# Mixer: weight casts behind an mLSTM head's decays, and tail steps of the modulation queue in the last units of output projections

## The chip, the cores and the metric

One NeuronCore of a Trainium2 chip runs the whole layer as one program. The metric is the device time of one execution in microseconds (us), the median of three runs. Engines are named as in the profile: PE (TensorE, matmuls), ACT (ScalarE), DVE (VectorE), POOL (GpSimd) and SP (SyncE, which here issues nearly all transfers). Each engine takes its own instructions in order, and waits on semaphores of others.

## The reference, cut to what matters

One layer for 256 tokens, width 2048, feed-forward width 5632, all in float32:

```python
ada = silu(c) @ w_ada + b_ada                 # nine vectors of 2048: sh1, sc1, g1, ... g3
sh1, sc1, g1, sh2, sc2, g2, sh3, sc3, g3 = split(ada, 9)
h = swiglu(modulate(x, sh1, sc1), ffn1_w_in, ffn1_w_out)
x = layernorm(ALPHA * x + 0.5 * (1 + g1) * h, ln1_g, ln1_b)
h = token_mixer(modulate(x, sh2, sc2), ...)   # 8 Fox attention heads, 4 mLSTM heads, w_out
x = layernorm(ALPHA * x + (1 + g2) * h, ln2_g, ln2_b)
h = swiglu(modulate(x, sh3, sc3), ffn2_w_in, ffn2_w_out)
x = layernorm(ALPHA * x + 0.5 * (1 + g3) * h, ln3_g, ln3_b)
```

`modulate(x, sh, sc)` is a layer norm without parameters, times (1 + sc), plus sh. An mLSTM head weighs its products q.k by decays: exponentials of differences of accumulated gates, cut to the causal triangle.

## The kernel before, in words

**Matrix products.** A float32 product is made of three matmuls in a reduced format (`mm3`, L398 to L401): each operand is split into `hi`, its cast, and `lo`, the rest. Activations are split once. Weights are split as they come: `load_w` (L368) issues a 1 MB transfer on SP into one of three `raw` buffers (L374), ACT casts each half of it to `hi` (L150, six buffers) and DVE subtracts to get `lo` (L151, six buffers). PE then uses both. So SP, ACT and DVE must keep ahead of PE, and each is in order. The argument `behind` of `load_w` names an instruction after which the cast and the subtraction of that tile must be issued.

**Stages.** FFN1 (in, out projection `f1`), a boundary with the layer norm and the next modulation, the mixer, its out projection `mx`, a second boundary, FFN2 (columns 2 to 9 in two halves, `fh` over the first half of the rows, `gf` and `fs` over the second), its out projection `f2`, and the last layer norm.

**Mixer.** In order: the o-gate columns (`mo`), the v columns (`fv`, `mv` with 520 columns, then `mv` with 512), the mLSTM q and k (`m`), the Fox q and k of heads 4 to 7 (`fb`, `fbk`), those of heads 0 to 3 (`fa`, `fak`), the rest of the Fox v (`fv`), then `mx`. Each of these has four units of one `raw` tile. Behind each unit stands `step()`: `pump(R_MX)` and up to three steps of side work (attention heads, mLSTM heads). `form_a_four` (L1111) makes the q and k blocks. `mlstm_head` (L1292) issues for a head: the matmuls `gb` (gate row) and `sps` (q.k), four ACT instructions `dm` (L1306, L1307: the decays), four DVE multiplies (L1308, L1309), and a step later the matmuls `nps`. `sps` has one buffer that all four heads share. Heads 0 and 1 lie in and behind the last `fb` unit, heads 2 and 3 between the `fbk` units.

**Modulation vectors.** The nine vectors of `ada` are computed beside all that, by `AdaQueue`, in units named (vector, column block). A unit has sixteen *rows*: a 512 KB transfer on SP (L184) into one of two buffers `ar`, and a DVE multiply-add (L163 for the first, L165). Then it has *tail* steps: `ahi` on ACT, `alo` on DVE, the pair of matmuls `bc` (L178) that sum over the partitions, and for shift and scale the DVE steps `dg`, reduce and add (L195 to L199). `pump(n)` adds n to `owed`, makes one tail step if there is one, and then one row for each whole number in `owed`. A new unit with a buffer of its own isn't started while a tail of such a unit is pending, and then the rows stay owed. `need(n)` makes steps at once until n units are done, and sets `owed` to zero each time it finds them not done. Rates per unit: 1.2 in FFN1, 1 in its out projection, 1.42 in the mixer and in `mx`, 1.05 and 0.6 in FFN2.

In the last column group of an out projection (`lastg`), the last four units aren't pumped. At the end of `f1`, `finish1` calls `need(6)`; the tail of unit (3, 3), which held back the next unit, isn't done by then, 3.25 rows are owed, and they are forgotten. `need(12)` ahead of `gf` likewise finds the tail of (6, 3) not done, and forgets 0.79.

**Order.** The program is written in an order, and a scheduler then sets the order of each engine from priorities and its own idea of durations; `tc.issue_after` and `tc.manual_schedule` bind it at some places.

Of the kernel before, what the change touches and what calls it, by code (L numbers as in the profile page):

```python
# [9 lines left out]
AF = mybir.ActivationFunctionType  # L10
# [22 lines left out]
def layer_kernel(  # L33
# [8 lines left out]
    V, S, G_, PE, SP = nc.vector, nc.scalar, nc.gpsimd, nc.tensor, nc.sync  # L42
# [98 lines left out]
    @contextmanager  # L141
    def pinned():
        with ExitStack() as s:
            for i in pin.values():
                s.enter_context(tc.issue_after(i))
            yield
# [67 lines left out]
    class AdaQueue:  # L214
# [19 lines left out]
        def row(self):  # L234
# [14 lines left out]
                self.rows = None  # L249
            return True  # L250

        def pump(self, n):
            self.owed += n
            with pinned():
                if self.tails:
                    self.tail()
            while self.owed >= 1:
                with pinned():
                    if not self.row():
                        break  # L260
                self.owed -= 1
# [169 lines left out]
    def out_proj(w, rows, nk, tag, npump, finish, before=None, turned=False, spare=None, fine=None):  # L431
# [12 lines left out]
        for width in (1024, 512, 512):  # L444
# [55 lines left out]
            for i, u in enumerate(us):  # L500
                hs = []
                if before:
                    before(u * kn)
                into = spare() if spare and lastg and i == nu - nheld else None
                for k in range(u * kn, u * kn + kn, 2):
                    hs += rows(k)
                for kk, hi, lo in load_w(w[u * kn * P:(u + 1) * kn * P, col:col + width], kn, width,
                                         f"{tag}o{col}_{u}", into=into):
                    arg = (u * kn + kk, *hs[kk], hi, lo)
                    if lastg and i >= nu - nheld or not lastg and i == nu - 1:  # L510
                        held.append(arg)
                    else:
                        for a in range(2):
                            if a and lastg and fine is not None:
                                products(a, [arg], nk - nheld * kn - 1)
                            else:
                                products(a, [arg])
                if not lastg and i == nu - 1:

                    late += [add_up(a, bs=(b,)) for b in range(nb) for a in range(2)]  # L520
                    products(0, held)
                    catch_up(2)
                    products(1, held)
                else:
                    catch_up(2)
                if not lastg or i < nu - 4:
                    npump()
            if lastg:
                catch_up(99)
                if fine is None:  # L530
                    finish(lambda a: products(a, held), add_up, st)
                else:
                    for _ in add_up(1, stats=False):
                        pass
                    outs = [mm_tile(f"o_{tag}last{c}") for c in range(2)]
                    finish(lambda a: half_products(outs) if a else products(0, held),
                           lambda a: add_halves(outs) if a else add_up(0), st)
            else:
                col += width
# [423 lines left out]
    W = w_in[0]  # L963
# [98 lines left out]
    def step():  # L1062
        pump(R_MX)
        advance(NP)
# [5 lines left out]


    emptied = [None]


    def cols_form_b(c0, col, ws, use, name, four=False):
# [35 lines left out]
    def form_a_four(c0, name, before_last=lambda: None):  # L1111
        ps = [mm_tile(f"pr_{name}{i}", True) for i in range(2)]
        for u in range(4):
            if u == 3:
                before_last()
            for k4, hi, lo in load_w(W[u * 512:(u + 1) * 512, c0:c0 + 512], 4, 512, f"{name}{u}"):
                k = 4 * u + k4
                for f in range(4):
                    fs = slice(f * P, (f + 1) * P)
                    mm3(ps[f // 2][:, f % 2 * T:(f % 2 + 1) * T], hi[:, fs], lo[:, fs], xhi[:, k, :], xlo[:, k, :],  # L1120
                        k + f % 2 == 0, k + f % 2 == KD)
            step()
        return [ps[f // 2][:, f % 2 * T:(f % 2 + 1) * T] for f in range(4)]

# [168 lines left out]
    def mlstm_head(o, h):  # L1293
        yield from wait(["gates", "conv1"] + [f"head{h - 2}"] * (h > 1) + [f"o{h - 1}"] * (h % 2))
        if h % 2:
            yield True
        qm, km = o[:, 0, :], o[:, 1, :]
        gb = aux_tile(f"gb{h}")
        sps = [fifth_tile(f"sps{h}")[:, :T], gb[:, T:T + P]]
        dm = mx.tile([P, T + P], F32, tag="dm", bufs=2, name=f"dm{h}")  # L1300
        PE.matmul(gb[:, :T], sel(h), ng, start=True, stop=True)
        for i in range(2):
            PE.matmul(sps[i], km[:, i * P:(i + 1) * P], qm[:, i * P:], start=True, stop=True)
        for i in range(2):
            d = dm[:, i * T:T + i * P]
            S.activation(d, gb[:, i * P:T], AF.Relu, bias=nacol[:, i, h:h + 1])  # L1306
            S.activation(d, d, AF.Exp, scale=-1.0)  # L1307
            V.tensor_tensor(out=d[:, :P], in0=d[:, :P], in1=triu1[:, :P], op=ALU.mult)  # L1308
            V.tensor_tensor(out=d, in0=sps[i], in1=d, op=ALU.mult)  # L1309
        done.add(f"o{h}")  # L1310
        yield
        yield True
        nps = [aux_tile(f"nps{h}{tt}") for tt in range(2)]
        for tt in range(2):
            PE.matmul(nps[tt][:, :MV + 1], dm[:, tt * P:(tt + 1) * P], yM[h][:, 0, :MV + 1],
                      start=True, stop=tt == 0)
        PE.matmul(nps[1][:, :MV + 1], dm[:, T:], yM[h][:, 1, :MV + 1], start=False, stop=True)
        for tt in range(2):
            dn = sm.tile([P, 2], F32, tag="dn", bufs=4, name=f"dn{h}{tt}")
            V.scalar_tensor_tensor(out=dn[:, 0:1], in0=nps[tt][:, MV:MV + 1], scalar=-1.0, in1=em[:, tt, h:h + 1],  # L1320
                                   op0=ALU.mult, op1=ALU.max)
            V.tensor_tensor(out=dn[:, 0:1], in0=nps[tt][:, MV:MV + 1], in1=dn[:, 0:1], op=ALU.max)
            V.reciprocal(dn[:, 1:2], dn[:, 0:1])
            S.mul(hm(h)[:, tt, :], nps[tt][:, :MV], dn[:, 1:2])
            S.activation(nps[tt][:, :MV], hm(h)[:, tt, :], AF.Square, accum_out=ss[:, tt, h:h + 1])
        done.add(f"head{h}")
        yield
# [183 lines left out]
    for j in range(2, 10):  # L1511
        if j == 8:
            for _ in mb:
                pass
        if j == 7:
            mb = late_features(2, 11)
        ps = half_in(j, 0, "fh")
        for f in range(2):
            i = 2 * j + f
            S.copy(hT[:, i, :], ps[f][:, :T])  # L1520
            S.copy(hT[:, i + 16, :], ps[f][:, T:])
# [71 lines left out]
```

## Time and profile before

| | us |
|---|---|
| median of three runs (lowest, highest) | 1929.29 (1928.31, 1930.26) |
| the profiled execution | 1927.28 |
| its span | 1925.6 |
| PE busy | 1891.5 (98%) |
| DVE busy | 1483.4 (77%) |
| ACT busy | 953.7 (50%) |
| mean granted clock of PE | 0.995 |

A row of a timeline has start, duration, engine, line, operation, out<-in, shapes, and how many of the kind follow each other; in brackets the idle time of the engine ahead of it, and what ended that. In a row of a window table each engine's busy time stands with its number of instructions, then PE's granted clock, the share of the DMA engines, and GB/s. Times of a transfer run from issue to landing.

### The profile page before, as it was taken

The numbers are of one execution on the slowest core, as the hardware profiler recorded it, in microseconds if no ns is written. First come the engines' busy times: TensorE is split into PE (matmuls) and PEld (weight loads), VectorE is DVE, ScalarE is ACT, GpSimd is POOL, SyncE is SP. The second block draws the span as 40 slices with busy tenths as digits, with TensorE's granted clock in tenths as the row PEclk, the third lists the DMA queues.
The fourth block names the chain that finished last, engine by engine and source line by source line (L and its number), as shares of the span: only waits on it lengthen the run. The fifth ranks groups of instructions, "written<-read, shape, count | busy, mean of one in ns | idle before, by whom it ended". The sixth has DMA issues, their size and how long they took to land.

```text
span 1925.6 us, 32413 instructions
## 1 busy us (share of the span) xinstructions
PE 1891.5 (98%) x13133; PEld 1724.6 (90%) x13133; DVE 1483.4 (77%) x1847; ACT 953.7 (50%) x1359; POOL 59.7 (3%) x88
## 2 busy tenths in 40 slices
PE   6999999999999999999999999999999999999997
PEld 3999999999988887699989886999999999988886
DVE  6788989877789898888988887867766655555776
ACT  3554454444454555845655645565444444444562
POOL 1111100000000000100000000000000000000000
PEclk9999999999999999999999999999999999999999
DMA  9978969999898787499988883987777766755552
GB/s 359 375 262 313 328 218 296 337 331 306 266 339 296 267 301 236 138 321 317 319 300 272 315 300 114 338 282 246 262 248 260 246 213 196 240 184 189 196 196 89
DMA packets 283662, 510.92 MB, mean 265 GB/s; under 512 B 10962, under 2 KB 134514, under 8 KB 282488
## 3 DMA queue, kind: packets, MB, share of 16 engines
q1 hardware_dynamic: 275640, 480.53, 73.4%
q0 software_dynamic: 7872, 28.32, 4.4%
q8 instruction: 103, 1.69, 0.4%
q14 instruction: 47, 0.39, 0.1%
HBM read 506.71 MB, written 2.10 MB: 264 GB/s over the span
## 4 chain that ended last, share of the span: by engine, by line
PE 84%; DVE 7%; DMA 5%; issue 2%; ACT 1%; SPq 0%; DVEq 0%; POOL 0%; ACTq 0%
PE gu_f L401 8%; PE gu_f L400 8%; PE gu_f L399 8%; PE o_f L399 6%; PE o_f L401 6%; PE o_f L400 6%; PE s L400 4%; PE s L399 4%; PE s L401 4%; DMA ar<-in_w_ada_dram 3%; PE fs L401 1%; PE fs L399 1%; PE fs L400 1%; PE o_mx L399 1%; PE o_mx L401 1%
## 5 line engine op out<-in xcount | busy, mean ns | idle before, releaser
L165 DVE SCALAR_TENSOR_TENSOR acc<-ar,csil,acc 128x1024 f32<-128x1024 f32 (+1 forms) x167 | 211.4, 1267 | 52.2 <-DMA ar<-in_w_ada_dram 51.5
L400 PE MATMUL s<-xlo_f,hi_s 128*128 128x256 f32 x768 | 213.6, 278 | 1.2 <-DVE xlo_f L331 1.2
L399 PE MATMUL s<-xhi_f,hi_s 128*128 128x256 f32 x768 | 213.4, 279 | 0.0
L401 PE MATMUL s<-xhi_f,lo_s 128*128 128x256 f32 x768 | 213.3, 278 | 0.0
L401 PE MATMUL gu_f<-xhi_f,lo_f2i 128*128 128x256 f32 x768 | 212.0, 276 | 0.0
L399 PE MATMUL gu_f<-xhi_f,hi_f2i 128*128 128x256 f32 x768 | 212.0, 276 | 0.0
L400 PE MATMUL gu_f<-xlo_f,hi_f2i 128*128 128x256 f32 x768 | 212.0, 276 | 0.0
L151 DVE TENSOR_TENSOR lo_f2i<-raw_f2i,hi_f2i 128x1024 fp32r<-128x1024 f32 x96 | 117.4, 1224 | 92.4 <-ACT hi_f2i L150 92.4
L401 PE MATMUL gu_f<-xhi_f,lo_f1i 128*128 128x256 f32 x640 | 176.7, 276 | 0.0
L399 PE MATMUL gu_f<-xhi_f,hi_f1i 128*128 128x256 f32 x640 | 176.7, 276 | 0.0
L400 PE MATMUL gu_f<-xlo_f,hi_f1i 128*128 128x256 f32 x640 | 176.7, 276 | 0.0
L150 ACT CAST hi_f2i<-raw_f2i 128x1024 fp32r<-128x1024 f32 x96 | 100.8, 1050 | 135.4 <-PE gu_f L400 124.6
L150 ACT CAST hi_s<-raw_s 128x1024 fp32r<-128x1024 f32 x96 | 100.6, 1052 | 130.3 <-PE s L400 93.4
L400 PEld LDWEIGHTS s<-xlo_f,hi_s 128*128 128x128 f32 x768 | 145.5, 189 | 1.5 <-DVE xlo_f L331 1.5
L401 PEld LDWEIGHTS s<-xhi_f,lo_s 128*128 128x128 f32 x768 | 145.4, 189 | 0.0
L399 PEld LDWEIGHTS s<-xhi_f,hi_s 128*128 128x128 f32 x768 | 144.9, 189 | 0.0
L399 PEld LDWEIGHTS gu_f<-xhi_f,hi_f2i 128*128 128x128 f32 x768 | 144.2, 188 | 0.2
L400 PEld LDWEIGHTS gu_f<-xlo_f,hi_f2i 128*128 128x128 f32 x768 | 144.2, 188 | 0.2
L401 PEld LDWEIGHTS gu_f<-xhi_f,lo_f2i 128*128 128x128 f32 x768 | 144.2, 188 | 0.0
L151 DVE TENSOR_TENSOR lo_f2o<-raw_f2o,hi_f2o 128x1024 fp32r<-128x1024 f32 x86 | 105.2, 1223 | 43.3 <-ACT hi_f2o L150 43.3
L165 DVE SCALAR_TENSOR_TENSOR gate<-ar,csil,gate 128x1024 f32<-128x1024 f32 (+1 forms) x94 | 117.5, 1251 | 25.4 <-DMA ar<-in_w_ada_dram 25.2
L151 DVE TENSOR_TENSOR lo_s<-raw_s,hi_s 128x1024 fp32r<-128x1024 f32 x96 | 115.5, 1219 | 27.4 <-ACT hi_s L150 27.2
(478 smaller groups left out, 5511.6 us busy)
## 6 DMA issues: line engine op xcount, KB each, us to landing
ar<-in_w_ada_dram SPq DMA_DIRECT2D x227, 512.0 KB, 5.4
raw_f2i<-in_ffn_w_in_dram SPq DMA_DIRECT2D x48, 1024.0 KB, 5.2
raw_s<-in_ffn_w_in_dram SPq DMA_DIRECT2D x47, 1024.0 KB, 7.6
raw_f1o<-in_ffn_w_out_dram SPq DMA_DIRECT2D x44, 1024.0 KB, 7.3
raw_f2o<-in_ffn_w_out_dram SPq DMA_DIRECT2D x44, 1024.0 KB, 5.1
raw_f1i<-in_ffn_w_in_dram SPq DMA_DIRECT2D x40, 1024.0 KB, 7.4
ar<-in_w_ada_dram POOLq DMA_DIRECT2D x48, 512.0 KB, 6.9
raw_mxo<-in_w_out_dram SPq DMA_DIRECT2D x16, 1024.0 KB, 6.0
```

Source lines behind the costliest of these rows:

```text
L150: S.copy(hi, src)
L151: return V.tensor_tensor(out=lo, in0=src, in1=hi.bitcast(F32), op=ALU.subtract)
L165: V.scalar_tensor_tensor(out=acc, in0=raw, scalar=csil[:, k:k + 1], in1=acc, op0=ALU.mult, op1=ALU.add)
L399: PE.matmul(o, ah, bh, start=start, stop=False)
L400: PE.matmul(o, ah, bl, start=False, stop=False)
L401: PE.matmul(o, al, bh, start=False, stop=stop)
```

## The change

A method `end_step` makes one tail step and no row. It is called in the last four units of an out projection's last column group, and once more in each of the last two columns of `fh`. And the casts and subtractions of a q or k block's unit are issued behind the decays of the mLSTM head that was recorded two units before.

```diff
+        def end_step(self):
+            if self.tails:
+                with pinned():
+                    self.tail()
+
         def pump(self, n):
             self.owed += n
-            with pinned():
-                if self.tails:
-                    self.tail()
+            self.end_step()
             while self.owed >= 1:
...
                 if not lastg or i < nu - 4:
                     npump()
+                else:
+                    ada.end_step()
...
     emptied = [None]
+    decays = [None, None]
...
-            for k4, hi, lo in load_w(W[u * 512:(u + 1) * 512, c0:c0 + 512], 4, 512, f"{name}{u}"):
+            for k4, hi, lo in load_w(W[u * 512:(u + 1) * 512, c0:c0 + 512], 4, 512, f"{name}{u}",
+                                     behind=decays[0]):
...
+            decays[:] = decays[1], None
             step()
...
-            S.activation(d, d, AF.Exp, scale=-1.0)
+            decays[1] = S.activation(d, d, AF.Exp, scale=-1.0).ins
...
         ps = half_in(j, 0, "fh")
+        if j >= 8:
+            ada.end_step()
```

All engines have as many instructions as before, and up to the first `mv` units (some 850 us into the span) they stand in the same order. The lists below are the order of the built programs; a digit right behind the letters of a name is left out (`ar_1_2` is row 2 of unit (6, 1), `bc_3_0` belongs to unit (6, 3)), and the last number of a name is the buffer's. Lines of the new program are 3 to 8 higher from L249 on.

ACT, at the mLSTM heads 0 and 1 (`dm` is written by the decays, `hi_fbk` by the casts for `fbk`), before:

```order
L150 CAST hi_fbk_10448<-raw_fbk_10446 128x1024
L150 CAST hi_fbk_10476<-raw_fbk_10446 128x1024
L150 CAST hi_fbk_10540<-raw_fbk_10538 128x1024
L150 CAST hi_fbk_10568<-raw_fbk_10538 128x1024
L1306 ACTIVATE dm_10354<-gb_10352,nacol 128x256
L1306 ACTIVATE dm_10354<-gb_10352,nacol 128x128
L1307 ACTIVATE dm_10354<-dm_10354 128x256
L1307 ACTIVATE dm_10354<-dm_10354 128x128
L150 CAST hi_fbk_10621<-raw_fbk_10619 128x1024
L1383 ACTIVATE qs_10711<-pr_fb_10121 128x256
L150 CAST hi_fbk_10649<-raw_fbk_10619 128x1024
L1306 ACTIVATE dm_10432<-gb_10430,nacol 128x256
```

and now:

```order
L1314 ACTIVATE dm_10366<-gb_10364,nacol 128x256
L1314 ACTIVATE dm_10366<-gb_10364,nacol 128x128
L1315 ACTIVATE dm_10366<-dm_10366 128x256
L1315 ACTIVATE dm_10366<-dm_10366 128x128
L150 CAST hi_fbk_10457<-raw_fbk_10455 128x1024
L150 CAST hi_fbk_10485<-raw_fbk_10455 128x1024
L1391 ACTIVATE qs_10720<-pr_fb_10140 128x256
L1314 ACTIVATE dm_10441<-gb_10439,nacol 128x256
L1314 ACTIVATE dm_10441<-gb_10439,nacol 128x128
L1315 ACTIVATE dm_10441<-dm_10441 128x256
L1315 ACTIVATE dm_10441<-dm_10441 128x128
L150 CAST hi_fbk_10549<-raw_fbk_10547 128x1024
```

The decays of head 0 moved ahead of the four casts for the first two units of `fbk`, and those of head 1 ahead of the second pair.

ACT again, at heads 2 and 3 (`yM` and `nps` end head 0), now:

```order
L1332 ACTIVATE yM_8728<-nps_10516,dn_10521 128x256
L1332 ACTIVATE yM_8728<-nps_10517,dn_10527 128x256
L1333 ACTIVATE nps_10516,ss<-yM_8728 128x256
L1333 ACTIVATE nps_10517,ss<-yM_8728 128x256
L1314 ACTIVATE dm_10535<-gb_10533,nacol 128x256
L1314 ACTIVATE dm_10535<-gb_10533,nacol 128x128
L1315 ACTIVATE dm_10535<-dm_10535 128x256
L1315 ACTIVATE dm_10535<-dm_10535 128x128
L150 CAST hi_fbk_10630<-raw_fbk_10628 128x1024
L150 CAST hi_fbk_10658<-raw_fbk_10628 128x1024
L1391 ACTIVATE qs_10724<-pr_fb_10141 128x256
```

Before, the casts `hi_fbk` of this unit stood ahead of head 2's L1306, and its L1307 behind `yM` and `nps`; now both casts stand behind all of that.

SP, the transfers around `mv`'s 512-column units, before:

```order
L184 DMA ar_1_0_9268<-in_w_ada_dram 128x2x512
L374 DMA raw_mv_0_9358<-in_w_in_dram 128x4x512
L184 DMA ar_1_1_9341<-in_w_ada_dram 128x2x512
L184 DMA ar_1_2_9392<-in_w_ada_dram 128x2x512
L374 DMA raw_mv_1_9401<-in_w_in_dram 128x4x512
L184 DMA ar_1_3_9445<-in_w_ada_dram 128x2x512
L374 DMA raw_mv_2_9466<-in_w_in_dram 128x4x512
L184 DMA ar_1_4_9448<-in_w_ada_dram 128x2x512
L374 DMA raw_mv_3_9519<-in_w_in_dram 128x4x512
L374 DMA raw_m_9572<-in_w_in_dram 128x4x512
```

and now:

```order
L184 DMA ar_1_0_9140<-in_w_ada_dram 128x2x512
L184 DMA ar_1_1_9209<-in_w_ada_dram 128x2x512
L377 DMA raw_mv_0_9377<-in_w_in_dram 128x4x512
L184 DMA ar_1_2_9288<-in_w_ada_dram 128x2x512
L184 DMA ar_1_3_9291<-in_w_ada_dram 128x2x512
L377 DMA raw_mv_1_9430<-in_w_in_dram 128x4x512
L184 DMA ar_1_4_9360<-in_w_ada_dram 128x2x512
L184 DMA ar_1_5_9418<-in_w_ada_dram 128x2x512
L377 DMA raw_mv_2_9482<-in_w_in_dram 128x4x512
L184 DMA ar_1_6_9421<-in_w_ada_dram 128x2x512
```

Two rows now stand ahead of each weight tile where before there were one or two.

DVE at the same place, before:

```order
L165 SCALAR_TENSOR_TENSOR gate<-ar_1_1_9341,csil,gate 128x1024
L151 TENSOR_TENSOR lo_mv_00_9361<-raw_mv_0_9358,hi_mv_00_9360 128x1024
L151 TENSOR_TENSOR lo_mv_01_9377<-raw_mv_0_9358,hi_mv_01_9376 128x1024
L165 SCALAR_TENSOR_TENSOR gate<-ar_1_2_9392,csil,gate 128x1024
L1217 TENSOR_TENSOR gz<-gz,gbias 128x4
L1216 TENSOR_TENSOR gz<-gz,gbias 128x4
L1217 TENSOR_TENSOR gz<-gz,gbias 128x4
L1216 TENSOR_TENSOR gz<-gz,gbias 128x4
L1096 SCALAR_TENSOR_TENSOR ab<-gz 128x24
L1099 TENSOR_SCALAR lg<-gz 128x24
L151 TENSOR_TENSOR lo_mv_10_9404<-raw_mv_1_9401,hi_mv_10_9403 128x1024
L151 TENSOR_TENSOR lo_mv_11_9420<-raw_mv_1_9401,hi_mv_11_9419 128x1024
```

and now, from the same tile on:

```order
L151 TENSOR_TENSOR lo_mv_01_9396<-raw_mv_0_9377,hi_mv_01_9395 128x1024
L151 TENSOR_TENSOR alo_0_1_9285<-acc_0_8574,ahi_0_1_9284 128x512
L165 SCALAR_TENSOR_TENSOR gate<-ar_1_4_9360,csil,gate 128x1024
L1224 TENSOR_TENSOR gz<-gz,gbias 128x4
L1225 TENSOR_TENSOR gz<-gz,gbias 128x4
L1224 TENSOR_TENSOR gz<-gz,gbias 128x4
L1225 TENSOR_TENSOR gz<-gz,gbias 128x4
L165 SCALAR_TENSOR_TENSOR gate<-ar_1_5_9418,csil,gate 128x1024
L1102 SCALAR_TENSOR_TENSOR ab<-gz 128x24
L1105 TENSOR_SCALAR lg<-gz 128x24
L151 TENSOR_TENSOR lo_mv_10_9433<-raw_mv_1_9430,hi_mv_10_9432 128x1024
L151 TENSOR_TENSOR lo_mv_11_9449<-raw_mv_1_9430,hi_mv_11_9448 128x1024
```

Ahead of `lo_mv_10` rows up to `ar_1_5` are taken, and before up to `ar_1_2`; from there to the end of `mx` DVE has three to five rows more ahead of each `lo` than before. From the start of `fh` on it is one more at first, and two or three from the end of its second column on.

## The prediction

> **What bounds the kernel now.** I read the page first, then the waits of TensorE, then timelines around its one large wait, and last the transfers and the distance between VectorE and TensorE in the mixer. From the page:
>
> ```profile
> span 1925.6 us, 32413 instructions
> PE 1891.5 (98%) x13133; PEld 1724.6 (90%) x13133; DVE 1483.4 (77%) x1847; ACT 953.7 (50%) x1359; POOL 59.7 (3%) x88
> PE 84%; DVE 7%; DMA 5%; issue 2%; ACT 1%; SPq 0%; DVEq 0%; POOL 0%; ACTq 0%
> ```
>
> TensorE is busy for 98% of the span, so only its waits can be saved, and any new wait of it is paid in full. From the list of its waits (total, times, longest) those that the change touches:
>
> ```profile
> PE sps L1303 <- DVE dm L1309: 4.1, 1, 4.1
> PE bc L178 <- DVE alo L151: 1.5, 2, 0.9
> PE bc L178 <- ACT ahi L150: 0.5, 1, 0.5
> ```
>
> The first is mLSTM head 1, whose products (`sps`) need the buffer that head 0's decays free. Its timeline, and the granted clock (the column before the DMA share) in three stretches:
>
> ```profile
> 974.36 0.70 PE L1303 MATMUL sps<-o 128*128 128x256 f32 x2 [4.10 <-DVE dm L1309]
> ...
> 974.00:976.00 2.00, 1.64 (x8) 1.59 (x9) 2.00 (x4) 0.54 (x2) 0.00 (x0) 0.75 1.02 379
> 976.00:978.00 2.00, 2.00 (x12) 2.00 (x11) 2.00 (x3) 0.97 (x4) 0.00 (x0) 0.50 1.06 410
> 978.00:980.00 2.00, 2.00 (x17) 2.00 (x17) 2.00 (x6) 0.42 (x1) 0.00 (x0) 0.90 0.95 277
> ```
>
> Behind the wait the clock is down: 2 us x (0.25 + 0.50 + 0.10) = 1.7 us more lost. The whole place costs 5.8 us. Why head 0's decays are late:
>
> ```profile
> 963.72 0.28 PE L1301 MATMUL gb<-ng,rowsel 128*128 128x256 f32 x1
> ...
> 962.38 2.00 ACT L150 CAST hi_fbk<-raw_fbk 128x1024 fp32r<-128x1024 f32 x2
> 966.32 2.00 ACT L150 CAST hi_fbk<-raw_fbk 128x1024 fp32r<-128x1024 f32 x2 [1.94 <-DMA raw_fbk<-in_w_in_dram]
> 968.23 0.72 ACT L1306 ACTIVATE dm<-gb,nacol 128x256 f32<-128x256 f32 x2
> ...
> 968.81 2.35 DVE L151 TENSOR_TENSOR lo_fbk<-raw_fbk,hi_fbk 128x1024 fp32r<-128x1024 f32 x2
> 974.23 0.28 DVE L1309 TENSOR_TENSOR dm<-gb,dm 128x128 f32<-128x128 f32 x1
> ```
>
> Their input `gb` stands ready at 964, but ScalarE first casts two tiles whose transfer comes at 966.32; VectorE's half then follows more weight work.
>
> **Term 1: casts behind the decays.** In the new order head 0's four ScalarE instructions stand ahead of all `fbk` casts. They can run from 964 and end near 966; VectorE's two multiplies end near 968, two ahead of TensorE's need at 970.26 (974.36 less 4.10). Gain 5.8 us. The casts held back have cover here: the last `fb` block stands between.
>
> For heads 2 and 3 the casts now stand behind a chain that starts late. Head 2 in the old order, and when TensorE first wants the `lo` of the block concerned:
>
> ```profile
> 988.02 0.61 ACT L1307 ACTIVATE dm<-dm 128x256 f32<-128x256 f32 x2
> ...
> 991.32 0.28 PE L401 MATMUL pr_fbk<-xhi_mx,lo_fbk 128*128 128x256 f32 x1
> ```
>
> Decays done at 988.63, a cast of 1.00 (2.00 for two, above), a `lo` of 1.18 (2.35 for two): 990.8, only 0.5 ahead. One `w_ada` row (1.28, below) in front of the `lo` makes 0.8 of wait, two make 2.1. Head 3's block is similarly placed. I take 2.0 for both, between 0 and 4.2.
>
> **Term 2: tail steps in the last units of the first output projection.** Alone they cost nothing: up to 850 us every engine's order is the same as before, the two small waits on `ahi` and `alo` of that place (0.5 and 0.9, above) included. What they do is keep `need(6)` from finding a tail, so `owed` is not set to zero. By the code 3.25 rows were dropped there, and now stay owed. Each row is a 512 KB transfer into one of two buffers and a VectorE multiply-add. The mixer has little room for them:
>
> ```profile
> L184 SPq DMA_DIRECT2D ar<-in_w_ada_dram x9: 367/368/368, 862.0 to 896.9; - x9
> L165 DVE SCALAR_TENSOR_TENSOR gate<-ar,csil,gate x6: 1276/1278/1284, 872.9 to 895.6; 128x1024 f32<-128x1024 f32 x6
>   DMA ar<-in_w_ada_dram: 3.9, 3
> DMA to landing us min/median/max: 4.2/5.6/6.8
> ...
> DMA  9899999989998958999999998999999999998678
> ```
>
> (These are the answer on tile `ar` between 860 and 900, and the DMA share there in fortieths.) A buffer goes round in 5.6 + 1.28 + 0.37 = 7.25 us, so two give a row each 3.6 us at best; VectorE waited for only 3 of 9 rows, so the others lay waiting for it: I add 0.2 and take 3.8. The nine issues were 4.36 apart. The weights cannot pass: SP issues in order, two rows now ahead of each raw tile, and VectorE takes rows and `lo` in order.
>
> First place, `lo_mv_10`. Rows of VectorE, and the matmul that reads the tile:
>
> ```profile
> 872.94 1.28 DVE L165 SCALAR_TENSOR_TENSOR gate<-ar,csil,gate 128x1024 f32<-128x1024 f32 x1 [1.72 <-DMA ar<-in_w_ada_dram]
> ...
> 883.41 0.39 PE L400 MATMUL b_mv<-lo_mv,xhi_mx 128*128 128x512 f32 x1
> ```
>
> The quoted row is `ar_1_1`. Now `ar_1_3`, `ar_1_4` and `ar_1_5` stand ahead of `lo_mv_10`. `ar_1_3` takes the buffer of `ar_1_1` at 874.22: landed 879.9, done 881.2; `ar_1_5` takes it next: landed 886.9, done 888.2; `lo_mv_10` 1.18 later, 889.4: 6.0 late. `ar_1_1` may itself come up to 1.7 earlier, since `raw_mv_0` now stands behind it: 4.3. With the least landing, 4.2, the same steps give 3.2, less 1.7: 1.5.
>
> Second place, the last `lo` of `fb`, read at 965.43:
>
> ```profile
> 960.45 1.27 DVE L165 SCALAR_TENSOR_TENSOR acc<-ar,csil,acc 128x1024 f32<-128x1024 f32 x1
> ...
> 965.43 0.28 PE L401 MATMUL pr_fb<-xhi_mx,lo_fb 128*128 128x256 f32 x1
> ...
> ar<-in_w_ada_dram SPq DMA_DIRECT2D x5, 512.0 KB, 6.1
> ...
> ar<-in_w_ada_dram SPq DMA_DIRECT2D x15, 512.0 KB, 4.7
> ```
>
> The quoted row is the 21st after `ar_1_1`, 87.5 us later. The new order has 25 ahead of that `lo`: 874.22 + 25 x 3.8 + 1.2 = 970.4, 5.0 late. With a landing of 6.1 (860 to 880) a row takes 4.07: 11.7 late; with 4.7 (935 to 995) 3.37: not late. A wait at the first place moves the second back, so the larger counts, not the sum. I take 6.5, between 5.0 and 11.7 and near the row of this very stretch; ends 1.5 and 11.7.
>
> **Term 3: rows kept at the second output projection and `need(12)`.** At `fh`'s start two more rows stand ahead of the seventh `lo_fh`:
>
> ```profile
> 1215.74 1.28 DVE L165 SCALAR_TENSOR_TENSOR gate<-ar,csil,gate 128x1024 f32<-128x1024 f32 x1
> ...
> 1223.13 0.28 PE L401 MATMUL fh<-xhi_f,lo_fh 128*128 128x256 f32 x1
> ```
>
> 1217.02 + 2 x 3.8 + 1.2 = 1225.8: 2.7 late; 0 to 3.5.
>
> **Term 4: tail matmuls inside products.** `bc_2` and `bc_3` move into the mixer's output projection and into `fh`. They need `ahi` and `alo`, now behind other work; nearest are two such waits in the first projection's end, 0.5 and 0.9: I take 1.4 once, 0 to 2.8 for both. In exchange the wait behind `need(12)` goes:
>
> ```profile
> 1300.41 0.50 PE L178 MATMUL bc<-alo,trir 128*128 128x512 f32 x1 [0.60 <-DVE alo L151]
> ```
>
> **Sum.** Gains 5.8 + 0.6 = 6.4; losses 2.0 + 6.5 + 2.7 + 1.4 = 12.6; net 6.2 us slower. The profiled run took 1927.28 (span 1925.6 and 1.7 around it), 2.0 under the median of 1929.29: 1933.5 on its scale, 1935.5 on the median's.
>
> The clock: 4.10 us of wait brought half clock, 0.9 did not. I put no loss of clock in the sum, as the 6.5 comes at several tiles. The Trainium skill (TensorE: Matmul & The Clock Gate, "What's actually happening") puts the limit at an idle window of about 3.4 us; the trace agrees with the 4.10. By it a single new wait of that length would add the 1.7 again: 1937.2.
>
> **Rivals.** (A) Other side: rows land fast enough. If a row takes 3.4 us or less (landing 4.7 or less), the second place is not late and the first loses 1.5. For it: landings are 4.7 from 935 on, and a waiting TensorE asks for less. Against: the share of 0.9 around 870 to 890. With 1.0 for all else, 6.4 - 2.5 = 3.9 faster: 1925.4. The Trainium skill (DMA: Bandwidth & Descriptors, "Anatomy of one DMA — SWDGE (gpsimd) path") fits 2.0 us plus bytes over 436 KB/us, by estimate 3.2 us for a row, on GpSimd's path; that would give A, but the 4.2 at least of this trace speaks against it.
>
> (B) The two sides cancel: 4.3 for the rows, 1 each for casts and `fh`, nothing for the tails: 1929.2.
>
> (C) Row after row takes 4.07 us: 11.7, with 4.2, 3.5 and 2.8, is 22.2, less 6.4: 15.8 slower, 1945.1. For it: the issues 4.36 apart.
>
> (D) The change doesn't do what it says: the rows ahead delay head 0's multiplies on VectorE by more than 2 us, and head 1 waits as before. Then 5.8 returns: 1941.3.
>
> **How the numbers follow.** 0.2% is 3.9 us, about what a measurement can tell from no change. Forecast (3.9 to 12 slower) 0.58; A 0.12; B, within 3.9 either way, 0.17; C 0.08; D 0.05. So faster 0.12, same 0.17, slower 0.71. The range leaves out A's lower half and C: 1927 to 1943.
>
> **What would show it.** Right: no `sps` wait on `dm` near 970; new TensorE waits on `lo_mv`, `lo_m` or `lo_fb` between 880 and 975, with VectorE idle for `ar` ahead of them; on `lo_fbk` or `hi_fa` behind L1307's counterpart; on `lo_fh` near 1223; no wait behind `need(12)`. Wrong: no new wait in the mixer (A), or half clock behind one (more than the sum). If an `ar` lands in 4.7 us or less at 870 to 890, term 2 is too large.

## The result

The changed kernel takes 1942.25 us (median of six runs, 1940.40 to 1949.45); the kernel before took 1929.56 us beside it (six runs, 1926.91 to 1933.45). The ratio is 1.007, with a 95% interval from 1.0051 to 1.0089: 12.7 us slower. The forecast was 1935.5, 6.2 us slower, in a range from 1927 to 1943. The direction held, and the time lies 0.75 us inside the range; the loss was twice as large as forecast.

### The profile after

The page of the changed kernel, and the rows of its list of TensorE waits that the change touches (total, times, longest; lines are 3 to 8 higher than before):

```profile
span 1938.7 us, 32387 instructions
PE 1897.7 (98%) x13133; PEld 1729.1 (89%) x13133; DVE 1483.8 (77%) x1847; ACT 949.4 (49%) x1359; POOL 60.6 (3%) x88
```

```profile
PE bc L178 <- DVE alo L151: 4.8, 2, 3.9
PE pr_m L404 <- DVE lo_m L151: 3.5, 3, 2.1
PE b_mv L403 <- DVE lo_mv L151: 1.9, 1, 1.9
PE fh L402 <- ACT hT2b L1503: 0.5, 1, 0.5
PE fh L404 <- DVE lo_fh L151: 0.5, 1, 0.5
PE pr_fa L404 <- DVE lo_fa L151: 0.2, 1, 0.2
```

The span grew by 13.1 us. The wait of `sps` on `dm` is gone, and in its place stand new waits on `lo` tiles and one on `alo`. The head's place, in the timeline of the changed kernel:

```profile
976.16 0.73 ACT L1314 ACTIVATE dm<-gb,nacol 128x256 f32<-128x256 f32 x2 [2.58 <-PE gb L1311]
979.31 0.28 DVE L1317 TENSOR_TENSOR dm<-gb,dm 128x128 f32<-128x128 f32 x1
981.55 0.60 PE L1311 MATMUL sps<-o 128*128 128x256 f32 x2
```

ScalarE waits for `gb` and takes the decays at once, VectorE's last multiply ends at 979.59, and `sps` of head 1 starts at 981.55 without a wait: two us of room, as forecast.

The first new wait, in the `mv` block. Rows of the timeline (VectorE, TensorE), and from the answer on tile `ar` between 860 and 900 how long its transfers took to land:

```profile
882.16 1.28 DVE L165 SCALAR_TENSOR_TENSOR gate<-ar,csil,gate 128x1024 f32<-128x1024 f32 x1
885.37 1.28 DVE L165 SCALAR_TENSOR_TENSOR gate<-ar,csil,gate 128x1024 f32<-128x1024 f32 x1 [1.64 <-DMA ar<-in_w_ada_dram]
886.75 2.35 DVE L151 TENSOR_TENSOR lo_mv<-raw_mv,hi_mv 128x1024 fp32r<-128x1024 f32 x2
...
888.02 0.65 PE L403 MATMUL b_mv<-lo_mv,xhi_mx 128*128 128x512 f32 x1 [1.89 <-DVE lo_mv L151]
```

```profile
DMA to landing us min/median/max: 4.0/4.5/6.3
```

VectorE sits idle for a row's transfer, then does the row, then the `lo` for which TensorE waits. The rows follow at 3.2 us, since the transfers land in 4.5 at the median here.

The `m` block shows a second way, through SP and ScalarE, and with its last two rows a third:

```profile
922.92 2.67 SPq L184 DMA_DIRECT2D ar<-in_w_ada_dram  x2
926.01 0.38 SPq L377 DMA_DIRECT2D raw_m<-in_w_in_dram  x1
...
934.28 1.05 ACT L150 CAST hi_m<-raw_m 128x1024 fp32r<-128x1024 f32 x1 [4.81 <-DMA raw_m<-in_w_in_dram]
...
935.37 1.22 DVE L151 TENSOR_TENSOR lo_m<-raw_m,hi_m 128x1024 fp32r<-128x1024 f32 x1 [3.27 <-ACT hi_m L150]
...
941.79 2.46 DVE L1281 SCALAR_TENSOR_TENSOR o<-u,hcol,o 128x256 f32<-128x256 f32 x6
944.17 2.35 DVE L151 TENSOR_TENSOR lo_m<-raw_m,hi_m 128x1024 fp32r<-128x1024 f32 x2
```

SP is held for 2.67 us by two rows, and only then issues the weights; they land 8.3 us later, ScalarE has waited 4.81 for them, and VectorE 3.27 for ScalarE. TensorE's three waits on `lo_m`, 3.5 us together, lie between 935.9 and 945.4. That chain ends in the first of them, 0.75 us. The longest, 2.08 us up to 945.43, is for the `lo` at 944.17: its cast began on ScalarE at 939.22, but on VectorE a row (at 940.59) and six steps of the mLSTM block (L1281) stand ahead of it. How much of this SP's order makes isn't shown by these rows: in the kernel before, SP also spends 2.70 and 2.77 us on pairs of rows at 913 and 920, and TensorE doesn't wait there.

The largest single wait is behind `fh`'s last products, for the second half of unit (6, 3):

```profile
1297.93 1.28 DVE L165 SCALAR_TENSOR_TENSOR gate<-ar,csil,gate 128x1024 f32<-128x1024 f32 x1 [1.00 <-DMA ar<-in_w_ada_dram]
1299.14 0.68 DVE L195 TENSOR_TENSOR dg<-bc,ident 128x512 f32<-128x512 f32 x1
1299.74 1.27 DVE L165 SCALAR_TENSOR_TENSOR gate<-ar,csil,gate 128x1024 f32<-128x1024 f32 x1
...
1301.53 0.68 DVE L151 TENSOR_TENSOR lo_gu<-raw_gu,hi_gu 128x512 fp32r<-128x512 f32 x1
1302.12 0.68 DVE L151 TENSOR_TENSOR alo<-gate,ahi 128x512 fp32r<-128x512 f32 x1
...
1302.86 0.79 PE L178 MATMUL bc<-alo,trir 128*128 128x512 f32 x1 [3.94 <-DVE alo L151]
```

`alo` stands on VectorE behind two rows, the tail work of the first half and a weight's `lo`; TensorE has the matmul that reads it in the middle of its products, and stands for 3.94 us.

Last, the granted clock (the number ahead of the DMA share) behind these waits:

```profile
888.00:890.00 2.00, 1.98 (x5) 1.59 (x6) 1.90 (x5) 1.99 (x4) 0.00 (x0) 0.55 0.84 301
890.00:892.00 2.00, 2.00 (x6) 1.52 (x6) 2.00 (x3) 0.42 (x1) 0.00 (x0) 0.59 1.05 389
...
946.00:948.00 2.00, 2.00 (x13) 2.00 (x12) 2.00 (x3) 0.50 (x1) 0.00 (x0) 0.56 0.95 336
948.00:950.00 2.00, 2.00 (x12) 2.00 (x12) 2.00 (x3) 1.41 (x2) 0.00 (x0) 0.59 0.83 273
...
1302.00:1304.00 2.00, 1.14 (x4) 1.04 (x5) 2.00 (x5) 0.00 (x0) 0.54 (x1) 0.50 0.90 314
1304.00:1306.00 2.00, 2.00 (x11) 2.00 (x10) 1.76 (x3) 0.00 (x0) 0.00 (x0) 0.50 0.65 136
1306.00:1308.00 2.00, 2.00 (x12) 2.00 (x11) 2.00 (x5) 0.00 (x0) 0.00 (x0) 0.50 0.83 192
```

Behind the wait of 1.9 the loss is 2 x (0.45 + 0.41) = 1.7 us, behind that of 2.1 it is 2 x (0.44 + 0.41) = 1.7, and behind that of 3.9 it is 2.6 (0.50 of the 1.14 us in which TensorE was busy in the first stretch, and 2 x 0.50 in each of the other two). Together 6.0 us of lost clock.

### Where the time went

| term | forecast, us | in the two profiled runs, us |
|---|---|---|
| head 1's wait and its half clock, gone | -5.8 | -5.8 |
| the wait behind `need(12)`, gone | -0.6 | -0.6 |
| casts behind late decays (`pr_fa`) | 2.0 | 0.2 |
| kept rows in the mixer (`b_mv` 1.9, `pr_m` 3.5) | 6.5 | 5.4 |
| kept rows at `fh` (0.5 and 0.5) | 2.7 | 1.0 |
| tail matmuls inside products (`bc` on `alo`) | 1.4 | 3.9 |
| half clock behind the new waits | 0 | 6.0 |
| sum | 6.2 | 10.1 |

Of the 13.1 us between the two spans, 3.0 are left. The same matmul near 802 us, ahead of all that the change moves, starts 1.6 us later in the changed kernel's profile; two runs of one order differ by as much there. The last 1.4 stays open.

Of the two waits at `fh`, neither is at the tile that the forecast worked out: one is at 1214.80, where TensorE waits for ScalarE, which had waited 1.60 us for the transfer of `raw_fh`, and the other at 1242.65.

### The profile page after: what moved, and what is told of

The parts are those of the page before. It is cut to its first block, busy times and chain, and to the rows that moved or that the text cites. A ratio compares the mean times of both kernels' runs of the same rounds, so it can differ in the third digit from the quotient of the medians.

```text
span 1938.7 us, 32387 instructions
## 1 busy us (share of the span) xinstructions
PE 1897.7 (98%) x13133; PEld 1729.1 (89%) x13133; DVE 1483.8 (77%) x1847; ACT 949.4 (49%) x1359; POOL 60.6 (3%) x88
## 4 chain that ended last, share of the span: by engine, by line
PE 81%; DMA 9%; DVE 6%; ACT 2%; issue 2%; SPq 0%; POOL 0%; DVEq 0%; ACTq 0%
PE gu_f L402 8%; PE gu_f L404 8%; PE gu_f L403 8%; PE o_f L402 7%; PE o_f L404 7%; PE o_f L403 7%; PE s L402 4%; PE s L403 4%; PE s L404 4%; DMA ar<-in_w_ada_dram 3%; DMA raw_fh<-in_ffn_w_in_dram 2%; PE fs L403 1%; PE fs L402 1%; PE fs L404 1%; PE o_mx L402 1%
```

## The experiments

The theory was: the rows that `need(6)` no longer drops make the loss, by holding up weight tiles; the casts bring a gain; the clock behind the new waits is what the forecast lacked (for this last part there is no run of its own; it rests on the clock rows above). In the quoted expectations an R with a number is a rival, told with what it expects. Differences are to the kernel before in the same runs, and the interval is that of the ratio.

### The two parts apart

e1_decays is the change without both calls of `end_step`; e2_tails is the change with the casts not held back; e5_keep_owed is the kernel before with nothing but the owed rows kept.

```diff
 e1_decays (against the changed kernel)
-                else:
-                    ada.end_step()
...
-        if j >= 8:
-            ada.end_step()
 e2_tails (against the changed kernel)
-                                     behind=decays[0]):
+                                     behind=None):
 e5_keep_owed (against the kernel before)
+        owed = ada.owed
         need(6)
+        ada.owed = owed
```

> Only the casts behind the decays; no tail step is added, so 3.25 rows are dropped as before. Theory (the change's loss lies in the kept rows and in bc_3_1, its gain in head 1): 5.8 us faster than before, about 1923.8; no wait of sps on dm, no new wait in the mixer, bc behind need(12) waits 0.6 as before. Rival R1 (casts held back behind late decays cost by themselves, 2 to 4 us at fbk and fa): 1 to 4 us faster, with waits of pr_fbk or pr_fa on hi or lo.

> Only the tail steps; the casts aren't held behind the decays. Theory: the losses stay and the gain goes: about 12.7 + 5.8 = 18 us slower than before, 1948; waits on lo_mv and lo_m of 5 us in all, on bc_3_1 of 4, and head 1's wait again. Rival R2 (rows ahead only hurt together with the held casts): within 3 us of before, no wait on lo_mv or lo_m.

> The kernel before, with one thing changed: need(6) at the first output projection's end leaves owed as it is (3.25). No added tail step, no cast behind decays. Theory (the kept rows alone make the loss): waits on lo_mv and lo_m of 3 to 5 us in all, head 1's wait on dm gone or small since TensorE comes later, 7 to 11 us slower than before: 1936 to 1940. Rival R3 (it takes the tail steps): within 2 us of before.

| | us (runs) | difference | ratio, 95% |
|---|---|---|---|
| e1_decays | 1923.29 (12) | -5.3 | 0.9966 to 0.9989 |
| e2_tails | 1939.14 (5) | +10.5 | 1.0043 to 1.0067 |
| e5_keep_owed | 1936.82 (12) | +7.9 | 1.0024 to 1.0050 |

The casts alone are a gain of 5.3 us, with one small new wait behind the late decays (a row of e1_decays' list of waits):

```profile
PE pr_fbk L404 <- DVE lo_fbk L151: 0.8, 1, 0.8
```

Kept rows alone, with no other edit, are a loss of 7.9 us, and make the waits of the changed kernel in the same blocks (e5_keep_owed, list of waits, and the stretch behind its longest wait, which ends at 942.91):

```profile
PE pr_m L401 <- DVE lo_m L151: 3.5, 3, 2.1
PE b_mv L400 <- DVE lo_mv L151: 3.2, 3, 1.5
```

```profile
944.00:946.00 2.00, 2.00 (x20) 2.00 (x19) 2.00 (x2) 0.00 (x0) 0.00 (x0) 1.00 0.85 271
```

So the kept rows are a cause by themselves. Two more things are to be seen. First, neither e2_tails nor e5_keep_owed has a wait of `sps` on `dm`, although their casts stand where they stood; e2_tails was expected to have it, and to lose 18 us. TensorE comes to that place 5.4 and 8.6 us later than before, and the decays end only 0.3 and 3.6 us later, so the wait is used up. The gain of the casts and the loss of the rows therefore don't add: -5.3 and +10.5 would be +5.2, and the change is +12.7. Beside kept rows the casts brought no gain that these runs show. Second, the wait of 2.1 us on `lo_m` is there in e5_keep_owed as in the changed kernel, and here no clock was lost behind it.

### The change without the kept rows

e3_owed0 is the whole change with the rows dropped after `need(6)` as before; e6_owed1 keeps at most 1.25 of them.

```diff
         need(6)
+        ada.owed = 0                       (e3_owed0)
+        ada.owed = min(ada.owed, 1.25)     (e6_owed1)
```

> The whole change, but owed is set to zero behind need(6), so that no row is kept from the first output projection; all tail steps stay. In its order DVE has as many rows ahead of every lo as the kernel before, but for one or two at fbk. Theory (it is the 3.25 kept rows): no wait on lo_mv and lo_m, none on lo_fh; gain 5.8 kept; bc_3_1 in fh has one row less ahead of it and waits 1 at most: 5 to 6 us faster than before, about 1924. Rival R3 (the tail steps themselves, in the last units, cost): still slower than before, by 3 us or more, with the waits in the mixer.

> The whole change, but at most 1.25 rows are kept from the first output projection, so that one to three more rows than before stand ahead of a lo in the mixer in place of three to five. Theory (the lead of lo over TensorE takes the first row, the loss begins behind it): no wait on lo_m over 0.5, head 1's gain kept, 2 to 4 us faster than before: 1925 to 1927. Rival R5 (every kept row costs its time): between the two ends in proportion, 1924.5 + 17.7 x 1.25 / 3.25 = 1931.

e3_owed0 takes 1924.53 us (8 runs): 4.1 faster than before, ratio 0.9964 to 0.9984. No wait on a `lo` is left in the mixer, none at `fh`, none behind `fh`'s products: it is the kept rows that also bring the wait for unit (6, 3), not the tail steps by themselves. One wait returned, 2.2 us of `sps` on `dm`, since on VectorE a row that waits 2.05 us for its transfer, and the end of a unit's tail (L195 to L199), stand ahead of head 0's multiplies (e3_owed0, timeline):

```profile
968.86 1.28 DVE L165 SCALAR_TENSOR_TENSOR acc<-ar,csil,acc 128x1024 f32<-128x1024 f32 x1 [2.05 <-DMA ar<-in_w_ada_dram]
970.06 0.68 DVE L195 TENSOR_TENSOR dg<-bc,ident 128x512 f32<-128x512 f32 x1
...
971.58 0.48 DVE L1317 TENSOR_TENSOR dm<-dm,trir 128x128 f32<-128x128 f32 x2
```

This is rival (D) of the prediction in a small form, not in the changed kernel but in one of its parts.

e6_owed1 missed what every theory expected: 1937.86 us (12 runs), 8.9 slower, 1.0028 to 1.0056, with 1.25 rows where 3.25 cost 12.7. Up to the end of `mv` nothing is lost (the first matmul of `pr_m` is at 902.54, before at 902.47), so with 1.25 rows the first place costs nothing. But other places came up (list of waits, and VectorE's timeline ahead of the first):

```profile
PE lps L1177 <- DVE gate L210: 3.5, 1, 3.5
PE pr_fb L404 <- DVE lo_fb L151: 2.0, 1, 2.0
```

```profile
1030.19 1.27 DVE L165 SCALAR_TENSOR_TENSOR gate<-ar,csil,gate 128x1024 f32<-128x1024 f32 x1
1031.39 1.21 DVE L151 TENSOR_TENSOR lo_fak<-raw_fak,hi_fak 128x1024 fp32r<-128x1024 f32 x1
1032.53 0.68 DVE L210 SCALAR_TENSOR_TENSOR gate<-bc,gate 128x512 f32<-128x512 f32 x1
```

The step L210 reads `bc`; a Fox head's `lps` comes from the same pool of buffers, so it waits until VectorE has got past a row and a `lo` to L210. How many rows are kept decides which unit's tail ends beside which head. Both waits brought half clock (1.7 us each). The cost of kept rows is thus not a price per row.

### The tail steps in `fh`

```diff
         ps = half_in(j, 0, "fh")
-        if j >= 8:
-            ada.end_step()
```

> The whole change without the two extra tail steps in fh's last columns, so that bc_3_0 and bc_3_1 stand at gf as before; the rows stay kept. Theory (bc_3_1's place costs 3.9 and a half clock of 3.4 behind it): waits in the mixer as in the changed kernel; the wait of 3.9 goes, 0.6 or a little more at need(12) returns: 6 to 7 us less than the changed kernel, about 1936. Rival R4 (alo comes late because of the rows kept, wherever the matmul stands): the wait only moves to gf, still 3 to 4 us with its half clock: within 2 us of 1942.

e4_no_fh takes 1939.28 us (5 runs), 10.6 slower, 1.0040 to 1.0064. Against the change's +12.7 that is 2.1 less, where 6.5 us of wait and clock stood at the place, so the result lies between the theory (1936) and the rival (within 2 us of 1942). The wait on `alo` is gone but for 0.3 us, and another came up at the start of `fs` (e4_no_fh, list of waits, and ScalarE's timeline):

```profile
PE fs L402 <- ACT hi_fs L150: 2.5, 1, 2.5
...
1318.54 2.00 ACT L150 CAST hi_fs<-raw_fs 128x1024 fp32r<-128x1024 f32 x2 [4.10 <-DMA raw_fs<-in_ffn_w_in_dram]
```

It begins near 1317, with 1.7 us of half clock behind it. On VectorE `alo` is as late as in the changed kernel (1303.72, there 1302.12), but TensorE now reads it behind `fh`'s products, at 1304.81. At `fs` it then meets a weight transfer that ScalarE waits for, 4.10 us. The place of the tail's matmul thus decides in part where TensorE loses the time.

### Rows behind the heads' multiplies

Rows and tail steps of the modulation queue are issued behind what stands in `pin`. Adding the last multiply of an mLSTM head's decays to it keeps them from standing ahead of it. e7_decays_pin is e1_decays with this, e8_owed0_pin is e3_owed0 with this.

```diff
-            V.tensor_tensor(out=d, in0=sps[i], in1=d, op=ALU.mult)
+            pin["d"] = V.tensor_tensor(out=d, in0=sps[i], in1=d, op=ALU.mult).ins
```

> Only the casts behind the decays, and w_ada rows recorded later are also issued behind the last multiply of an mLSTM head's decays on VectorE (with the casts alone a row that waits for its transfer stands ahead of head 0's multiplies). Theory: head 0's multiplies end near 967 in every run, so no run has head 1's wait: 6 to 7 us faster than before, 1922, and no slower than the casts alone. Rival R6 (rows held back make the next tail or lo late): 1 to 3 us slower than the casts alone.

> The whole change with owed set to zero behind need(6), and rows behind the heads' multiplies as in the run with the casts. In the profile without that order head 1 still waited 2.18 with 1.7 of clock behind it, as a row that waited 2.05 for its transfer stood ahead of head 0's multiplies. Theory: that goes, 7 to 8 us faster than before, about 1921. Rival R6: as slow as without it, 1924.5, with a new wait behind it.

e7_decays_pin takes 1921.16 us (10 runs; 0.9947 to 0.9977), e8_owed0_pin 1920.40 us (7 runs; 0.9933 to 0.9968): 7.8 and 8.5 us faster than before. Both beat both kernels; between the two the intervals don't tell. In neither profile does TensorE wait for as much as 1 us in the mixer, and no clock is lost there. So the change's own idea is sound: with the rows dropped as before, and kept off the multiplies, it is worth 8 us. What the order on VectorE would give without the held casts, no run shows.

### What sets the pace of the rows

My reason had three parts that could be at fault: SP's order, a row's landing, VectorE's time. e9_rows_pool is the change, e10_before_pool the kernel before and e11_keep_pool is e5_keep_owed, each with the rows issued on POOL from the end of the first output projection on, so that SP has only weights to issue.

```diff
         need(6)
+        rowq[0] = G_
...
-            SP.dma_start(raw, src[k * P:(k + 1) * P])
+            rowq[0].dma_start(raw, src[k * P:(k + 1) * P])
```

> The whole change, but from the end of the first output projection on the rows of the modulation queue are issued on POOL instead of SP, so no weight transfer stands behind a row that waits for its buffer. Theory (the kept rows cost time because SP issues in order, and weights wait behind rows): the waits on lo_mv, lo_m and lo_fb between 880 and 975 go from 5.4 us to under 2, without half clock, and the kernel is at most 5 us above its own counterpart without the change, e10_before_pool. Rival (VectorE takes rows and lo in order, and a row's two buffers and its landing alone set the pace): the waits stay at 4 to 7 us, and the kernel is 9 to 14 us above e10_before_pool.

> The kernel before with its rows issued on POOL from the same place on: the base for e9_rows_pool and e11_keep_pool. Both theories: no kept rows, so nothing new in the mixer; between 1926 and 1934 us. If POOL's issues were slow themselves, rows would land later and the time would rise; the difference to e9_rows_pool is what counts.

> e10_before_pool with the 3.25 rows kept, and nothing else of the change (e5_keep_owed with its rows on POOL). Theory (SP's order): 0 to 3 us above e10_before_pool, where e5_keep_owed was 7.9 above before. Rival (VectorE's order and the two buffers): 5 to 9 us above.

They take 1967.63, 1955.49 and 1961.97 us (5, 4 and 4 runs; before 1928.33). The base itself lost 27 us, so the queue is no neutral place to put the rows. The times are those of the rival: the change stands 12.1 above its base and the kept rows 6.5, much as on SP (12.7 and 7.9). The waits are those of the theory: between 880 and 975 TensorE waits for no `lo` in e9_rows_pool, and loses no clock. The difference of 12.1 comes from other places on both sides: e9_rows_pool waits 6.7 us for `yF` at 874 and 5.2 for `alo` at 1329, and its base waits 6.5 for head 0's decays at 1003. So this trial decides nothing about SP's order, which stays open.

Next, half the cost of a row, once in bytes and once in VectorE's time, each beside the kernel before with the same edit.

```diff
 e12_half_bytes, e13_before_half_bytes (a3, r3, s3: acc, raw and source as two halves)
-            SP.dma_start(raw, src[k * P:(k + 1) * P])
-            ada_acc(acc, raw, k)
+            SP.dma_start(r3[:, :1], s3[:, :1])
+            ada_acc(a3, r3[:, :1].to_broadcast([P, 2, 512]), k)
 e14_half_mults, e15_before_half_mults (all rows of a unit but its first)
-            ada_acc(acc, raw, k)
+            ada_acc(a3[:, :1], r3[:, :1], k)
```

> The whole change, with half the bytes of each row from the end of the first output projection on (256 KB; VectorE still works 1024 columns, the first half twice, so the vectors of units from there on are wrong by that). Theory (a row's landing in two buffers sets the pace of the kept rows): rows land in about 3 to 4 us instead of 4 to 6.3, the waits on lo_mv and lo_m in the mixer fall from 5.4 to under 2, bc_3_1's from 3.9 to under 2, and the kernel is at most 3 us above e13_before_half_bytes, or below it. Rival (VectorE's time for a row and its order): waits of 4 us or more stay in the mixer and the difference stays at 9 to 13 us.

> The kernel before with the same halved transfers: base for e12_half_bytes. Theory and rival: within 4 us of before, since TensorE is the bound there, with head 1's wait of 4.1 us perhaps shorter as fbk's transfer lands earlier.

> The whole change, with VectorE's multiply-add of a row (but the first of a unit) on half the columns from the same place on, the transfers whole (the second half of these vectors lacks 15 of 16 rows). Theory (landing sets the pace): of 1.28 us some 0.55 go per row, 3.25 kept rows are 1.8 us, so 2 to 4 us of waits stay in the mixer and the difference to e15 is 6 to 12 us. Rival (VectorE's time): mixer waits under 1.5 us and a difference of 3 us or less.

> The kernel before with the same halved multiply-adds: base for e14_half_mults. Theory and rival: 0 to 5 us below before, as head 0's multiplies stand behind less work on VectorE and head 1's wait of 4.1 shrinks.

| | with the change | without | the change is worth |
|---|---|---|---|
| as it is | 1942.25 | 1929.56 | +12.7 |
| half the bytes (e12, e13) | 1918.80 | 1928.07 | -9.3 |
| half VectorE's time (e14, e15) | 1926.38 | 1927.59 | -1.2 |

(6 and 12 runs for the second line, 12 and 12 for the third.) TensorE's order is that of the changed kernel, or of the one before; on VectorE, ScalarE and SP the scheduler moved some instructions, since a row's length enters its rules, so the halving isn't the only difference. The kept rows are still there: ahead of each of the sixteen `lo` tiles of `m`, VectorE has done as many rows in e12 and e14 as in the changed kernel, give or take one, and three to five more than in the kernel before. With half the bytes no wait is left in the mixer, at `fh` or behind its products. With half of VectorE's time these are left (e14_half_mults, list of waits):

```profile
PE bc L178 <- DVE alo L151: 1.7, 2, 1.1
PE pr_m L410 <- DVE lo_m L151: 1.5, 1, 1.5
```

Each base takes nearly the time of the kernel before, but not with the same waits. Head 1's wait, which the change takes away, has another length in them (e13_before_half_bytes, then e15_before_half_mults):

```profile
PE sps L1312 <- DVE dm L1318: 7.2, 1, 7.2
PE sps L1310 <- DVE dm L1316: 3.5, 1, 3.5
```

With the clock lost behind it, 2.5 and 3.0 us, that place costs 9.7 and 6.5 us, where it cost 5.8 before; a shorter wait was expected in both, and with half the bytes it is longer. So the last column of the table is a gain at head 1 and a cost of the rest together. By this sum (an estimate from the rows) the rest costs 18.5 us as it is, 0.4 with half the bytes, and 5.3 with half of VectorE's time.

How long the transfers take between 860 and 950 tells more of the bytes. These are the rows (`ar`, up to 900) and the weights (`raw_m`) in e12_half_bytes, and then `raw_m` in the changed kernel:

```profile
DMA to landing us min/median/max: 3.1/4.5/5.4
DMA to landing us min/median/max: 5.1/5.2/7.3
DMA to landing us min/median/max: 6.5/7.7/9.3
```

A halved row lands in 4.5 us at the median, as a whole row does in the changed kernel, where 3 to 4 was expected. What lands sooner is the weights: 5.2 us and not 7.7. So it is the kept rows' use of the transfers first, which the weights share, and VectorE's time as well: taking either away brings most tiles back into their room of a few us. That a `lo` is late by the sum of what stands ahead of it fits both, but is not shown tile by tile. Neither the theory (landing alone) nor its rival (VectorE alone) holds as it was put. e12 met the theory's waits and time, but not its landing; e14 fell between the two (2.6 us of waits in the mixer's blocks and heads where the theory had 2 to 4, but a difference of -1.2 where it had 6 to 12).

## Why the prediction was right and wrong

**The gain** was right in size and in its mechanism: 5.8 us at head 1, with the room of two us in front of it, and 0.6 behind `need(12)`. What the prediction didn't see is that the kept rows take away the same wait without the casts (e2, e5).

**Kept rows as the cause** was right: e3 and e5 show it from both sides. The size of the mixer's waits, 6.5, was near the measured 5.4, but by luck, for the steps to it were not the ones that happened. At `mv` the wait was 1.9 where 4.3 to 6.0 was worked out, because rows landed in 4.5 at the median and followed at 3.2 us instead of 3.8. The second place was to be the last `lo` of `fb`; it was the `m` block, behind a weight transfer that came late and behind a row and mLSTM steps on VectorE. And the two places added, where I let the larger count alone.

**"I put no loss of clock in the sum"** is the step that failed. The reason given, that the 6.5 comes at several tiles, was right about the tiles and wrong about the clock: waits of 1.9 and 2.1 us brought 1.7 us of half clock each, the one of 3.9 brought 2.6. The measured loss is 6.5 us over the forecast (12.7 - 6.2): the clock makes 6.0 of that, the waits together came out 2.1 below the forecast, and the other 2.6 no row explains (1.6 us of difference stands ahead of all that the change moves). The trace of before had shown 0.9 without and 4.10 with half clock; everything between was open, and I took the harmless end without giving the other end to the sum. That half clock behind a new wait would mean more than the sum, the prediction said itself, as a sign of being wrong. The range held the result, but its upper end was set by late rows and not by the clock. The figure of the Trainium skill that I set beside it (TensorE: Matmul & The Clock Gate, "What's actually happening": an idle window of about 3.4 us) supported that end; the trace doesn't agree, with half clock behind 1.9 and 2.1.

**Term 4** was too small: 1.4 taken, 2.8 as its upper end, 3.9 measured, and its half clock beside it. The nearest rows (0.5 and 0.9) were of a place where the modulation queue had little backlog; this one had rows late, and `alo` stands behind them.

**Terms 1 and 3** were too large: 0.2 for 2.0, and 1.0 for 2.7. TensorE comes later to these places by what it lost before (5 to 7 us between the two profiles); that the casts and `lo` tiles get this as room fits, but no run tests it alone. I had used this argument between the first and the second place of term 2, and not for the terms behind it.

**The rivals.** (A) and (B) are excluded by the interval. (C) has a time near the measured one, 15.8 slower, but not by its mechanism: at the place where it was to cost 11.7 us, the last `lo` of `fb`, TensorE doesn't wait at all. (D) is no part of the changed kernel, but e3_owed0 has it.

The errors of the waits themselves partly cancel: -1.8 for term 1, -1.1 for term 2, -1.7 for term 3, +2.5 for term 4, together -2.1. So the waits alone would have made the loss smaller than forecast; the half clock turned it the other way.

## What to carry to other kernels

Where TensorE is the bound, price a new wait at its length and at a stretch of half clock behind it (1.7 us here), as soon as it may reach 2 us, and give the case with the half clock a place in the range where it may reach 1. Look at what an edit does to bookkeeping beside its purpose: here a queue's tail ended earlier, so a rule that dropped 3.25 rows no longer did, and undoing that side effect turned a loss of 12.7 us into a gain of 4.1, or of 8.5 with the rows issued behind the heads' multiplies. And don't add a gain and a loss that lie on one path: a bound engine that is late already finds no wait to save further on.

## What was not expected of the hardware

Half clock comes in stretches of one length, or of twice that. The loss behind the head's wait in the kernel before, behind 1.9 and 2.1 in the changed kernel, and behind both waits of e6_owed1 is 1.7 us each time, which is 3.4 us at a granted clock of 0.50. Behind the wait of 3.9 the clock was down twice as long, some 6.8 us, begun in the wait itself (0.81 in the stretch from 1300 to 1302, then 0.50 for six us), and so it was behind the 3.5 of e15_before_half_mults; behind 4.6 us at the same `bc` in e2_tails it was down for one length only.

What starts a stretch isn't the length of the wait alone. The same 2.1 us on `lo_m` brought one in the changed kernel and in e2_tails, and none in e5_keep_owed, whose row stands above at 1.00, nor in e4_no_fh. And a wait of 1.0 us in FFN1, at a place that the change doesn't touch, brought one in e4_no_fh and none in e3_owed0 (for each the matmul that waited, then the clock after it; e4_no_fh first):

```profile
170.04 0.61 PE L790 MATMUL cp<-trir,gate 128*128 128x1 f32 x4 [1.03 <-DVE gate L165]
171.00:173.00 2.00, 2.00 (x11) 2.00 (x12) 2.00 (x5) 1.05 (x3) 0.67 (x1) 0.54 1.00 379
```

```profile
171.06 0.61 PE L790 MATMUL cp<-trir,gate 128*128 128x1 f32 x4 [1.04 <-DVE gate L165]
172.00:174.00 2.00, 2.00 (x20) 2.00 (x20) 2.00 (x5) 1.03 (x3) 0.69 (x1) 1.00 0.99 383
```

So at 1.0 and at 2.1 us the same wait goes both ways. In the two kernels and in e1 to e6, each wait of 2.2 us or more behind FFN1's start brought half clock, but that is no limit either: in e10_before_pool 2.57 us on `lo_m`, up to 954.69, brought none (1.00 in every stretch of 2 us from 950 to 968). The Trainium skill (TensorE: Matmul & The Clock Gate, "What's actually happening") speaks of an activity window that runs free of the program, of about 3.4 us; the stretches agree with that length, and that the same wait goes both ways would fit it. The figure of the Trainium skill for what it takes, an idle window of about 3.4 us, does not agree with 1.0 and 1.9.

Issuing the rows on POOL instead of SP from the end of the first output projection on cost the kernel before 27 us (e10_before_pool); its profile shows longer waits at the heads and at `lo` tiles, and the mechanism stays open.
